# The last pair of each feed-forward's first part as seven block products

## The chip, the cores and the metric

One core of a Trainium2 chip runs the whole program. The metric is the device time of one execution in microseconds (us), as the median of several runs of the same kernel.

## What is computed

Two layers on 512 tokens of width 1024. Layer 0 has a causal convolution module, layer 1 differential attention; each is followed by a SwiGLU feed-forward network with a hidden width of 2816 and by a gated per-layer embedding. Only the two feed-forwards matter here:

```python
def swiglu(x, w_gate, w_up, w_down):
    return (jax.nn.silu(x @ w_gate) * (x @ w_up)) @ w_down

u = rms_norm(h, ffn_norm_g[i])
h = h + swiglu(u, ffn_w_gate[i], ffn_w_up[i], ffn_w_down[i])
```

All values are float32. The kernel splits every operand of a product into a rounded part (hi) and the rest (lo), and a product is three matmuls: hi by lo, lo by hi, hi by hi (`mm3`, lines 162 to 165).

## The kernel before

The activations stand with the features on the 128 partitions and the 512 tokens along the free axis, so a width of 1024 is 8 chunks of 128 x 512, and the hidden width is 22 chunks. `ffn` (it begins at line 572) takes these 22 chunks in three parts of 8, 8 and 6 (`PARTS`). A part makes its hidden chunks two at a time, a **pair**; with pairs written as (part, number) there are (0,0) to (0,3), (1,0) to (1,3) and (2,0) to (2,2), eleven in all. Then `linear` multiplies the part's chunks by the down weights and adds the result to `h` (lines 758 and 759). This second half of a part is called the down product here.

An **ordinary pair** makes, for each of its two chunks, the gate product and the up product from eight input chunks: four weights of 128 x 1024, and 4 x 8 x 3 = 96 matmuls of 512 columns. Each weight is loaded by SyncE's queue (L153), rounded on ScalarE (L156, the hi part) and its rest taken on VectorE (L158, the lo part).

A **seven-product pair** (those listed in `SEVEN`) makes the same two chunks by Strassen's scheme: input features, hidden features and tokens are each cut into two halves, and seven block products with a contraction over four chunks and 256 tokens take the place of eight. `strassen` runs once for the gate and once for the up weights, with 7 x 4 x 3 = 84 matmuls of 256 columns each, 168 for a pair. Two kinds of operands feed it:

- `comb`, sums and differences of blocks of the activations. Blocks 1, 2 and 3 are the normed activations themselves; 5, 7, 6 and 4 are made by the generator `normed` (lines 618 to 622, on VectorE and ScalarE). They are written into the tiles A, which hold the raw input `norm.u` until the last raw pair has read it.
- `operands`, sums and differences of blocks of the weights: a difference q, made by a plain load on SyncE's queue (L649) and an accumulating DMA on GpSimd's queue (L650); a raw block r (L652); a smaller block z (L654, tile `bias`); two sums s2 and s4 on VectorE (L666, L667). All of them are split by `split` (L642 on ScalarE, L643 on VectorE) into the ring of four hi and four lo tiles that the ordinary weights use as well.

The seven products run in the order 1, 5, 7, 2, 6, 4, 3; product 1 needs r, products 5 and 7 need q.

The first two ordinary pairs read `norm.u`, unnormed, and scale their results by the row factors `rb`. The later ordinary pairs read the normed tiles `un`. The generator `normed` first makes the eight normed chunks (lines 592 to 599) and then, once the raw pairs are done, the eight steps of `comb`. `feed(n)` lets it take n steps; the table `STEPS` says how many after each half of an ordinary pair, and 2 is taken where the table ends.

The order of instructions on each engine is fixed when the program is built: a scheduler places them from the order of the code and its own estimates. On the chip each engine then works through its list in order.

The sources of the normed chunks are kept in three tiles of the kinds that q uses (`qtags`: C5, C5, C4 in layer 0, C2, C3, C4 in layer 1), and in `wth`, which s2 uses. So the first q in such a tile can be loaded only when the steps of `comb` that read the old content have run.

Of the kernel before, what the change touches and what calls it, by code (L numbers as in the profile page):

```python
# [23 lines left out]
NC = D // P  # L24
# [58 lines left out]
    (("C2", "C3", "C4"), [(t,) for t in ("C0", "C0", "C1", "C1", "C5", "C5")] + [("D0", "D1"), ("D4", "D5")]),  # L83
)
RAW_PAIRS = 2
STEPS = (0, 2, 3, 3)
SEVEN = ((1,0),(1,1),(1,2),(1,3),(2,0),(2,1),(2,2))
QKV = (("q", 0, (0, 0, 0, 0)), ("v", 0, (0, 1, 1, 0)), ("q", 1, (1, 1, 2, 2)), ("q", 2, (0, 1, 2, 0)), ("v", 1, (1, 2, 2, 2)), ("q", 3, (0, 2, 0, 1)))


# [1 line left out]
def trunk(ctx, tc, xT, pT, wts, diag, dww, vec, rel, onehot, lamv, out):  # L92
# [9 lines left out]
    def sb(shape, tag, bufs, dt=F32):  # L102
        uid[0] += 1
        return pool.tile(shape, dt, tag=tag, name=f"{tag}_{uid[0]}", bufs=bufs)
# [40 lines left out]
    def weight(n=1024, pieces=1, between=(), eng=V, after=None):  # L145
        i = wnext[0]
        wnext[0] += 1
        raw = sb([P, 1024], "wraw", 2)
        hi = sb([P, 1024], "whi", 4, F32R)
        lo = sb([P, 1024], "wlo", 4, F32R)  # L150
        for k in range(pieces):
            cut = slice(k * n // pieces, (k + 1) * n // pieces)
            loaded[0] = nc.sync.dma_start(raw[:, cut], wts[i, :, cut])  # L153
            if k < len(between):
                between[k]()
            A.copy(hi[:, cut], raw[:, cut])  # L156
            with tc.issue_after(after.ins) if after else nullcontext():
                eng.tensor_tensor(lo[:, cut], raw[:, cut], f(hi[:, cut]), ALU.subtract)  # L158
        return hi, lo

    def mm3(acc, a, b, first, last):
        (ah, al), (bh, bl) = a, b
        T.matmul(acc, al, bh, start=first, stop=False)  # L163
        T.matmul(acc, ah, bl, start=False, stop=False)  # L164
        return T.matmul(acc, ah, bh, start=False, stop=last)  # L165

    def wpart(w, k):
        return tuple(t[:, k * P : (k + 1) * P] for t in w)
# [377 lines left out]
    def linear(n_in, src, consume, group0=1, before=None, after=None, first=(None,) * 3):  # L546


        m = 0
        while m < NC:  # L550
            g = group0 if m == 0 else 1
            ws = [weight(n_in * P, after=first[i] if m == 0 else None) for i in range(g)]
            accs = [mm() for _ in range(g)]
            for k in range(n_in):
                if before:
                    before(k)
                for w_, a_ in zip(ws, accs):
                    mm3(a_, wpart(w_, k), src[k], k == 0, k == n_in - 1)
                    if after:
                        after()  # L560
            for i in range(g):
                consume(m + i, accs[i])
            m += g
# [10 lines left out]
    def ffn(norm, after, space):  # L574
        qtags, utags = space
        rb = None
        un = []
        comb = {}
        uses = [None]
# [46 lines left out]
        making = [normed()]  # L626

        def feed(n=1):
            for _ in range(n):
                if making:  # L630
                    try:
                        next(making[0])
                    except StopIteration:
                        making.pop()
# [42 lines left out]
        def strassen(i):  # L677

            w = operands(i)

            def product(acc, name):
                for k in range(4):
                    mm3(acc, wpart(w[name], k), comb[name][k], k == 0, k == 3)

            one, two, three, four = sc(), mm(), mm(), tp()
            t, e, g = wk(), big(), big()
            first, second = slice(0, H2), slice(H2, S)
            product(one[:, first], 1)
            A.copy(t[:, first], one[:, first])
            A.mul(t[:, second], one[:, first], -1.0)  # L690
            product(three[:, first], 5)
            product(three[:, second], 7)
            product(two[:, first], 2)
            product(two[:, second], 6)
            V.tensor_tensor(e, two, t, ALU.add)
            V.tensor_tensor(
                g.rearrange("p (a s) -> p a s", a=2), three.rearrange("p (a s) -> p a s", a=2),
                e[:, second].unsqueeze(1).to_broadcast([P, 2, H2]), ALU.add,
            )
            V.tensor_tensor(e[:, second], three[:, second], g[:, first], ALU.add)  # L700
            product(four[:, second], 4)
            V.tensor_tensor(g[:, second], four[:, second], g[:, second], ALU.add)
            product(four[:, first], 3)
            V.tensor_tensor(g[:, first], four[:, first], g[:, first], ALU.subtract)
            return e, g

        seen = 0
        for at, (f0, n) in enumerate(PARTS):
            hid = []
            for pair in range(n // 2):  # L710
                hi, lo = (sb([P, 2, S], f"B{2 * pair + k}", 1, F32R) for k in range(2))
                for k in range(2):
                    hid.append((hi[:, k], lo[:, k]))
                if (at, pair) in SEVEN:
                    i = wnext[0]
                    wnext[0] += 4
                    gs = strassen(i)
                    for t in gs:
                        A.activation(t, t, AF.Silu)
                    us = strassen(i + 1)  # L720
                    for o, (t, g) in enumerate(zip(us, gs)):
                        V.tensor_tensor(t, t, g, ALU.mult)
                        first, step = (H2, H2) if o else (0, S + H2)
                        hs, ls = (bass.AP(x.tensor, x.offset + first, [list(x.ap[0]), [step, 2], [1, H2]]) for x in (hi, lo))
                        A.copy(hs, t.rearrange("p (a s) -> p a s", a=2))
                        V.tensor_tensor(ls, t.rearrange("p (a s) -> p a s", a=2), f(hs), ALU.subtract)
                    continue
                x = norm.u if seen < RAW_PAIRS else un
                for i in range(2):
                    wg, wu = weight(), weight()  # L730
                    pg, pu = mm(), mm()
                    for k in range(NC):
                        mm3(pg, wpart(wg, k), x[k], k == 0, k == NC - 1)
                    if rb is None:
                        norm.diagonal()
                    for k in range(NC):
                        mm3(pu, wpart(wu, k), x[k], k == 0, k == NC - 1)
                    if rb is None:
                        rb = norm.rows()
                    tg, tu = big(), big()  # L740
                    if x is un:
                        A.activation(tg, pg, AF.Silu)
                        V.tensor_tensor(tu, pu, tg, ALU.mult)
                    else:
                        V.tensor_tensor(tg, pg, rb, ALU.mult)
                        A.activation(tg, tg, AF.Silu)
                        V.tensor_tensor(tu, pu, rb, ALU.mult)
                        V.tensor_tensor(tu, tu, tg, ALU.mult)
                    A.copy(hi[:, i], tu)
                    V.tensor_tensor(lo[:, i], tu, f(hi[:, i]), ALU.subtract)  # L750
                    feed(STEPS[2 * seen + i] if 2 * seen + i < len(STEPS) else 2)
                seen += 1
                if seen == RAW_PAIRS:
                    assert len(un) == NC, len(un)
                    feed()
                    uses[0] = None

            def add(m, acc):
                V.tensor_tensor(h[m], acc, h[m], ALU.add)  # L759
                if at == len(PARTS) - 1:  # L760
                    after.chunk(m)

            linear(n, hid, add, 2)
# [28 lines left out]

    n2 = Norm("ple_g0")
    ffn(norm, n2, SPACE[0])
    norm = Norm("attn_g")
    ple(n2, pp, lambda m, cut: norm.chunk(m))
# [281 lines left out]
    linear(NC, ot, add_attn, 2, heads_until, step)  # L1078
    n2 = Norm("ple_g1")
    ffn(norm, n2, SPACE[1])  # L1080

    def store(m, cut):
# [130 lines left out]
```

## Time and profile before

| | us |
|---|---|
| median of three runs | 1290.93 |
| lowest and highest run | 1288.16, 1292.81 |
| the profiled execution | 1288.43 |
| its span, first to last instruction | 1286.3 |

The profiled execution is 2.1 us longer than its span. PE is TensorE's matmul, PEld its weight load, DVE is VectorE, ACT ScalarE, POOL GpSimd and SP SyncE, whose queue issues most DMAs. A row of the windows view gives, for one stretch of the span, its length, the busy time of each engine with the number of instructions, the granted clock of TensorE, the share of the DMA engines' time in use, and the GB/s. A row of the timeline gives the start, the time taken, the engine, the line, the operation, the tiles (out<-in) and the shapes; in brackets stands the idle time before it and what ended it. Rows of one kind that follow one another are merged into one with a count.

### The profile page before, as it was taken

The page shows a single profiled execution, that of the slowest core. Times are in us where ns is not written, and L with a number is a line of the kernel's source. Part 1 is how long each engine was busy: PE and PEld are TensorE (multiplying, and loading weights), DVE is VectorE, ACT ScalarE, POOL GpSimd, SP SyncE. Part 2 cuts the span into 40 slices and gives each one's busy share as a digit, 9 for nine tenths or more (in the row PEclk, how much of TensorE's full clock was granted, in tenths as well). Part 3 has the DMA queues.
Part 4 walks back from the last instruction along what each step waited for, and adds up shares of the span by engine and source line. Part 5 has one row for each costly group of instructions (what it writes and reads, how often), then busy time and mean ns, then how long its engine had stood idle before and what let it go on. Part 6 is the DMA issues. An engine that isn't in the chain of part 4 may idle for free. (4 is left out here: it accounts for less than half of the span.)

```text
span 1286.3 us, 18032 instructions
## 1 busy us (share of the span) xinstructions
PE 1253.5 (97%) x6912; PEld 1082.9 (84%) x6912; DVE 886.0 (69%) x1430; ACT 603.9 (47%) x999; POOL 268.4 (21%) x235
## 2 busy tenths in 40 slices
PE   8999999999999999999999997999999999999998
PEld 5888678888899989988888886778888899899887
DVE  6988647773478558766678887846953588558665
ACT  5642455442155325454566766734532255225442
POOL 4644323000000000033435534122000001000030
PEclk8999989999999999999999999999999999999999
DMA  6745314272456545243222221313463366444241
GB/s 228 226 154 167 116 49 116 81 213 82 115 155 174 148 123 134 69 127 104 80 87 92 83 64 50 98 49 116 119 175 99 105 172 175 136 113 117 81 137 66
DMA packets 58498, 154.15 MB, mean 120 GB/s; under 512 B 6275, under 2 KB 10883, under 8 KB 58412
## 3 DMA queue, kind: packets, MB, share of 16 engines
q1 hardware_dynamic: 52256, 134.89, 32.6%
q0 software_dynamic: 4032, 14.68, 6.9%
q10 hardware_dynamic: 2124, 3.43, 0.8%
q8 instruction: 54, 0.88, 0.3%
q14 instruction: 32, 0.26, 0.1%
HBM read 148.77 MB, written 4.21 MB: 119 GB/s over the span
## 5 line engine op out<-in xcount | busy, mean ns | idle before, releaser
L163 PE MATMUL mm<-A,wlo 128*128 128x512 f32 (+1 forms) x856 | 295.2, 350 | 5.6 <-ACT A L177 2.6
L164 PE MATMUL mm<-A,whi 128*128 128x512 f32 (+1 forms) x856 | 298.6, 350 | 0.3
L165 PE MATMUL mm<-A,whi 128*128 128x512 f32 (+1 forms) x856 | 296.5, 347 | 0.0
L156 ACT CAST whi<-wraw 128x1024 fp32r<-128x1024 f32 (+2 forms) x158 | 159.5, 1016 | 253.6 <-PE mm L165 120.0
L158 DVE TENSOR_TENSOR wlo<-wraw,whi 128x1024 fp32r<-128x1024 f32 (+2 forms) x154 | 196.3, 1278 | 86.3 <-ACT whi L156 86.1
L163 PEld LDWEIGHTS mm<-A,wlo 128*128 128x128 f32 x856 | 162.8, 190 | 28.5 <-DVE wlo L158 3.9
L164 PEld LDWEIGHTS mm<-A,whi 128*128 128x128 f32 x856 | 162.9, 190 | 24.2 <-DVE A L178 3.5
L165 PEld LDWEIGHTS mm<-A,whi 128*128 128x128 f32 x856 | 162.8, 190 | 20.6 <-issue 1.0
L164 PE MATMUL mm<-B,whi 128*128 128x512 f32 x352 | 137.2, 391 | 0.0
L165 PE MATMUL mm<-B,whi 128*128 128x512 f32 x352 | 137.1, 390 | 0.0
L163 PE MATMUL mm<-B,wlo 128*128 128x512 f32 x352 | 135.9, 392 | 0.0
L650 POOL DMA_DIRECT2D C<-in_wts x28 | 24.6, 878 | 520.0 <-DVE h L759 228.9
L197 POOL TENSOR_TENSOR acc<-acc,wk 128x512 f32<-128x512 f32 x42 | 66.1, 1574 | 229.2 <-ACT wk L196 121.2
L759 DVE TENSOR_TENSOR h<-mm,h 128x512 f32<-128x512 f32 x48 | 33.0, 688 | 75.2 <-PE mm L165 75.1
L165 PEld LDWEIGHTS mm<-B,whi 128*128 128x128 f32 x352 | 66.1, 188 | 14.5
L164 PEld LDWEIGHTS mm<-B,whi 128*128 128x128 f32 x352 | 66.1, 188 | 14.1
L163 PEld LDWEIGHTS mm<-B,wlo 128*128 128x128 f32 x352 | 66.1, 188 | 14.0
L165 PE MATMUL mm<-whi,A 128*128 128x512 f32 x192 | 75.7, 395 | 0.0
L164 PE MATMUL mm<-wlo,A 128*128 128x512 f32 x192 | 74.9, 395 | 0.0
L163 PE MATMUL mm<-whi,A 128*128 128x512 f32 x192 | 74.8, 396 | 0.0
L163 PE MATMUL mm<-C,wlo 128*128 128x512 f32 (+1 forms) x212 | 74.1, 350 | 0.0
L164 PE MATMUL mm<-C,whi 128*128 128x512 f32 (+1 forms) x212 | 73.8, 348 | 0.0
(269 smaller groups left out, 2593.8 us busy)
## 6 DMA issues: line engine op xcount, KB each, us to landing
wraw<-in_wts SPq DMA_DIRECT2D x166, 512.0 KB, 3.7
C<-in_wts SPq DMA_DIRECT2D x28, 512.0 KB, 4.5
C<-in_wts POOLq DMA_DIRECT2D x28, 512.0 KB, 6.0
bias<-in_wts SPq DMA_DIRECT2D x28, 256.0 KB, 3.6
wraw<-in_wts SPq DMA_DIRECT2D x16, 384.0 KB, 3.1
D<-in_diag SPq DMA_DIRECT2D x22, 256.0 KB, 4.8
C<-in_diag SPq DMA_DIRECT2D x16, 256.0 KB, 4.7
h<-in_xT SPq DMA_DIRECT2D x8, 256.0 KB, 5.8
```

What stands on the lines that cost most here:

```text
L156: A.copy(hi[:, cut], raw[:, cut])
L158: eng.tensor_tensor(lo[:, cut], raw[:, cut], f(hi[:, cut]), ALU.subtract)
L163: T.matmul(acc, al, bh, start=first, stop=False)
L164: T.matmul(acc, ah, bl, start=False, stop=False)
L165: return T.matmul(acc, ah, bh, start=False, stop=last)
L197: self.last = self.eng.tensor_tensor(self.acc, self.acc, sq, ALU.add)
L650: nc.gpsimd.dma_start(q, wts[i + 2].rearrange("p (a s) -> p a s", a=2), accum_op=ALU.add)
L759: V.tensor_tensor(h[m], acc, h[m], ALU.add)
```

## The change

The pair (0,3) of each feed-forward joins the list `SEVEN`, so that eight of eleven pairs are seven-product pairs and three are ordinary: (0,0) and (0,1) on the raw input, (0,2) on the normed one. `STEPS` now feeds the eight normed chunks during the first two pairs (2, 2, 2 and 3 steps) and the eight steps of `comb` during pair (0,2) (4 and 5 steps). Two loops take the place of a fixed assumption: what is left of `normed` is fed before the first seven-product pair, and before the raw tiles are given up.

```diff
 RAW_PAIRS = 2
-STEPS = (0, 2, 3, 3)
-SEVEN = ((1,0),(1,1),(1,2),(1,3),(2,0),(2,1),(2,2))
+STEPS = (2, 2, 2, 3, 4, 5)
+SEVEN = ((0,3),(1,0),(1,1),(1,2),(1,3),(2,0),(2,1),(2,2))
...
                 if (at, pair) in SEVEN:
+                    while making:
+                        feed()
                     i = wnext[0]
                     wnext[0] += 4
                     gs = strassen(i)
...
                 if seen == RAW_PAIRS:
-                    assert len(un) == NC, len(un)
-                    feed()
+                    while uses[0] is not un:
+                        feed()
                     uses[0] = None
```

In layer 1, VectorE's list around the end of pair (0,2) and the start of (0,3) reads before as follows (names with A are tiles of `comb`, B the hidden chunks, wlo the weights' rests; L743 multiplies a chunk's up product by its gate, L750 is the rest of a hidden chunk):

```order
L743 TENSOR_TENSOR big_8608<-mm_8558,big_8607 128x512
L158 TENSOR_TENSOR wlo_8719<-wraw_8717,whi_8718 128x1024
L622 TENSOR_TENSOR A_1721_8872<-wk_8868,A_1720_8871 128x512
L750 TENSOR_TENSOR B_1655_8544<-big_8608,B_1654_8543 128x512
L158 TENSOR_TENSOR wlo_8796<-wraw_8794,whi_8795 128x1024
L743 TENSOR_TENSOR big_8691<-mm_8641,big_8690 128x512
```

and after the change (lines from 716 on have moved down by two, so L745 and L752 are L743 and L750 of before):

```order
L745 TENSOR_TENSOR big_8734<-mm_8684,big_8733 128x512
L622 TENSOR_TENSOR A_1719_8860<-wk_8856,A_1718_8859 128x512
L752 TENSOR_TENSOR B_1675_8670<-big_8734,B_1674_8669 128x512
L666 TENSOR_TENSOR wth_8880<-C_1722_8865,wraw_8868 128x512
L666 TENSOR_TENSOR wth_9009<-C_1742_8994,wraw_8997 128x512
L667 TENSOR_TENSOR wtl_8881<-wth_8880,wraw_8868 128x512
L643 TENSOR_TENSOR wlo_8877<-C_1722_8865,whi_8876 128x1024
L667 TENSOR_TENSOR wtl_9010<-wth_9009,wraw_8997 128x512
L643 TENSOR_TENSOR wlo_8885<-wth_8880,whi_8884 128x512
L643 TENSOR_TENSOR wlo_8885<-wtl_8881,whi_8884 128x512
L745 TENSOR_TENSOR big_8830<-mm_8780,big_8829 128x512
```

The last step of `comb` (L622) keeps its place. The first sum of the new pair (L666) now stands behind it, and it reads the new pair's first q, the tile C_1722; everything below it in the list comes after that.

SyncE's list at the same place in layer 1, before (C tiles are the q blocks, L153 the ordinary weights):

```order
L649 DMA C_1798_9397<-in_wts 128x2x512
L153 DMA wraw_8634<-in_wts 128x1024
L649 DMA C_1776_9262<-in_wts 128x2x512
L153 DMA wraw_8711<-in_wts 128x1024
L153 DMA wraw_8717<-in_wts 128x1024
L649 DMA C_1756_9133<-in_wts 128x2x512
L153 DMA wraw_8794<-in_wts 128x1024
L153 DMA wraw_8800<-in_wts 128x1024
```

and after the change:

```order
L649 DMA C_1796_9385<-in_wts 128x2x512
L153 DMA wraw_8773<-in_wts 128x1024
L649 DMA C_1742_8994<-in_wts 128x2x512
L652 DMA wraw_8868<-in_wts 128x1024
L652 DMA wraw_8997<-in_wts 128x1024
L649 DMA C_1722_8865<-in_wts 128x2x512
L153 DMA wraw_9127<-in_wts 128x1024
L649 DMA C_1816_9514<-in_wts 128x2x512
```

The three q blocks are loaded at the same places as before. The two loads of raw blocks (L652) stand where two ordinary weights stood. The third q, which fed the seven-product pair after a whole down product, is now the first operand of the pair that follows at once. Outside pair (0,3) and the down product behind it, the five lists of both layers are the same as before but for a few neighbours on VectorE and ScalarE that have changed places.

## The prediction

> **What bounds the kernel now.** First the page's busy shares and its slices, to see whether one engine carries the whole span.
>
> ```profile
> PE 1253.5 (97%) x6912; PEld 1082.9 (84%) x6912; DVE 886.0 (69%) x1430; ACT 603.9 (47%) x999; POOL 268.4 (21%) x235
> PE   8999999999999999999999997999999999999998
> PEclk8999989999999999999999999999999999999999
> ```
>
> TensorE is busy for 97% of the span, and in nearly every slice for nine tenths or more, at the full granted clock but for two slices near the start. An average over stages is not yet a bound in the stage that changes, so next the windows view, cut at the borders of the pairs. I took the borders from TensorE's timeline, where the first matmul of each kind starts.
>
> ```profile
> core 0: us, PE busy (x) PEld busy (x) DVE busy (x) ACT busy (x) POOL busy (x), PEclk, DMA share, GB/s
> 264.62:286.38 21.76, 21.76 (x97) 18.02 (x96) 14.79 (x25) 8.61 (x12) 1.75 (x2) 1.00 0.86 215
> 286.38:308.14 21.76, 21.76 (x97) 18.02 (x96) 7.49 (x8) 6.22 (x8) 0.00 (x0) 1.00 0.31 98
> 308.14:352.16 44.02, 44.02 (x194) 36.05 (x192) 19.42 (x24) 8.93 (x10) 0.87 (x1) 1.00 0.33 98
> 352.16:372.31 20.15, 20.15 (x169) 20.15 (x168) 13.11 (x19) 9.98 (x16) 0.87 (x1) 1.00 0.52 129
> 352.16:432.69 80.53, 79.81 (x662) 79.35 (x660) 63.09 (x97) 42.56 (x68) 6.13 (x7) 1.00 0.63 162
> 432.69:478.18 45.49, 45.49 (x207) 37.49 (x205) 24.05 (x32) 10.60 (x12) 0.87 (x1) 1.00 0.45 130
> 478.18:537.38 59.20, 59.20 (x494) 59.08 (x493) 45.27 (x69) 30.87 (x50) 1.74 (x2) 1.00 0.37 102
> 929.96:951.72 21.76, 21.76 (x97) 18.02 (x96) 14.85 (x25) 8.62 (x12) 2.03 (x3) 1.00 0.83 214
> 951.72:973.48 21.76, 21.76 (x97) 18.02 (x96) 7.49 (x8) 6.21 (x8) 0.00 (x0) 1.00 0.30 92
> 1017.50:1037.65 20.15, 20.15 (x169) 20.15 (x168) 13.11 (x19) 9.98 (x16) 0.86 (x1) 1.00 0.49 127
> ```
>
> In order: pair (0,2) of layer 0, pair (0,3), the down product of that part, the seven-product pair (1,0), all four seven-product pairs of part 1, the down product behind them, the three pairs of part 2; then (0,2), (0,3) and (1,0) of layer 1. (A count may hold one matmul of the neighbouring window.) In every row but one TensorE is busy for the whole length, and the exception loses 0.72 of 80.53 us. So these stages are bound by TensorE, and what the change is worth is what it does to TensorE's list, as long as no operand comes late.
>
> **Pair (0,3) itself.** It takes 21.76 us in both layers: 96 matmuls at a pace of 0.227 us. A seven-product pair issues 168 matmuls of half the columns. Where operands are on time it takes 20.15 us, in both layers, a pace of 0.120 us. The change turns the first into the second once in each layer: 21.76 - 20.15 = 1.61 us, twice, **3.2 us**. Note how little is left of the 12.5% that seven for eight promises: a matmul of half the width takes 0.120 and not 0.113 us, and 168 x 0.120 stands against 96 x 0.227. PEld, the weight load, is busy for all of the 20.15 us, while it has 3.7 us to spare in the ordinary pair, so it may be what sets the pace.
>
> Seven-product pairs do not always run at that pace. Part 1 of layer 0 spends 80.53 us on 660 matmuls (0.1220), part 2 59.20 on 494 (0.1198). Over 168 matmuls these give 20.50 and 20.13, so a pair is worth between 1.26 and 1.63 us, and the two between 2.5 and 3.3. The slow bound contains one wait for a weight split:
>
> ```profile
> 413.90 0.36 PE L163 MATMUL mm<-A,wlo 128*128 128x256 f32 x1 [0.72 <-DVE wlo L643]
> ```
>
> I take 20.15, the row of the two pairs that, like (0,3), are the first of their run.
>
> **The down product behind it.** TensorE's list lets the last product of a seven-product pair (12 matmuls) run inside the following down product, among its first matmuls, as it does after part 1 now. That row, 45.49 us, less 12 x 0.12 = 1.44, leaves 44.05, against 44.02 behind an ordinary pair. I charge 0.03 per layer, **0.1 us** in all.
>
> **The steps that move.** The normed chunks and the steps of `comb` have another table, but VectorE's list keeps them at the places where they stand, so nothing is paid or won there. The matmuls of pairs (0,0) to (0,2) are the same and in the same order.
>
> **The first operands.** Before, q was loaded far ahead, and a whole down product lay between the end of `comb` and the first seven-product pair. Now pair (0,3) follows at once, and product 5, which is 12 x 0.12 = 1.44 us behind the pair's start, needs q. The chain is: the last reader of the old tile on VectorE, the plain load (SyncE), the accumulating load (GpSimd), the sums and the split on VectorE. In layer 1 it is tightest, because there the tile of the first q holds normed chunks that `comb` reads until its seventh step:
>
> ```profile
> 936.05 0.74 DVE L618 TENSOR_TENSOR wk<-C,wk 128x256 f32<-128x256 f32 x2
> 936.88 0.38 SPq L649 DMA_DIRECT2D C<-in_wts  x1
> 942.33 0.86 POOL L650 DMA_DIRECT2D C<-in_wts  x1 [9.08 <-DVE big L743]
> 943.87 0.68 DVE L750 TENSOR_TENSOR B<-big,B 128x512 fp32r<-128x512 f32 x1
> 948.11 1.22 DVE L158 TENSOR_TENSOR wlo<-wraw,whi 128x1024 fp32r<-128x1024 f32 x1 [3.55 <-ACT whi L156]
> DMA to landing us min/median/max: 5.7/5.7/5.7
> DMA to landing us min/median/max: 5.2/6.0/9.1
> DMA to landing us min/median/max: 4.8/4.8/4.8
> DMA to landing us min/median/max: 3.6/4.5/6.0
> ```
>
> The landing rows are those of this accumulating load, of all 28, of this plain load, and of all 28. The plain load starts right behind the reader, at 936.88, and takes 4.8 us. The accumulating load starts at 942.33 and lands 5.7 us later: 948.0. VectorE is idle from 944.5 to 948.1, so it reaches the first sum (L666) when q lands. Behind that stand, in its list, two more sums and then the rest of q:
>
> ```profile
> L643 DVE TENSOR_TENSOR wlo<-C,whi 128x1024 fp32r<-128x1024 f32 x7 | 8.5, 1218 | 0.4 <-ACT whi L642 0.4
> L667 DVE TENSOR_TENSOR wtl<-wth,wraw 128x512 f32<-128x512 f32 x5 | 3.4, 688 | 0.1
> L666 DVE TENSOR_TENSOR wth<-C,wraw 128x512 f32<-128x512 f32 x5 | 3.4, 685 | 3.5 <-DMA wraw<-in_wts 3.5
> ```
>
> 3 x 0.69 + 1.22 = 3.3, so q is ready at 951.3; ScalarE's rounding of q runs beside the sums. Product 5 wants it at 951.72 + 1.44 = 953.16. **1.9 us to spare.** In this time two ordinary weights that were loaded beside the accumulating load (SyncE's list has two L153 behind the q) are gone or wait for a free raw tile, so q lands earlier rather than later. The new wait stands at the head of VectorE's list. Queued behind it are the other splits of the pair; the sums are wanted by product 6, which starts 5.76 us into the pair, at 957.5, and they end at about 953.5. By the slowest landing, 9.1 us, q lands at 951.4 and is split at 954.7: 1.5 us late. Nothing earlier than in time can be won, so the bounds are 0 and 1.5 us; I take 0, by this load's own row.
>
> In layer 0 the tiles are free earlier:
>
> ```profile
> 263.43 1.05 POOL L650 DMA_DIRECT2D C<-in_wts  x1 [32.83 <-ACT A L621]
> 266.78 0.88 POOL L650 DMA_DIRECT2D C<-in_wts  x1 [2.29 <-DVE wk L618]
> ```
>
> Even at 9.1 us both first q blocks have landed by 275.9, more than ten us before pair (0,3) starts at 286.38. I charge nothing.
>
> **VectorE and the DMAs as a whole.** Pairs (0,2) and (0,3) have VectorE busy for 14.8 + 7.5 = 22.3 us of 43.5. A seven-product pair costs it 63.09 / 4 = 15.8 us in part 1, so the two would come to some 31 of 41.9. The transfers have room too: pair (0,3) uses 0.31 of the DMA engines and would go to about 0.63, the share of part 1.
>
> **The sum.** -3.2 + 0.1 = -3.1 us. Against the profiled execution that is 1288.43 - 3.1 = 1285.3, of which the span is 1283.2 and 2.1 lie around it. The median of the runs shown stands 2.5 us above the profiled execution; from it, 1290.93 - 3.1 = **1287.8 us**, 0.24% less. A measurement of this kernel tells about 0.3% (3.9 us) from no change, since its runs spread over 4.65 us, so a real gain of this size is likelier to be called the same than faster.
>
> **The rivals.** (1) *The first q is late.* TensorE then waits at product 5 of layer 1: 1.5 us with the slowest accumulating load, and 1.2 more if the plain load before it takes 6.0 instead of 4.8 us. The time is then 1289.3 to 1290.5. For it speaks that accumulating loads took up to 9.1 us where three of them crowded (263 us); against it that this one has already been seen at 5.7 us among two weight loads. [...]
>
> (2) *Slower than before.* The same place, but a landing so late that it eats the whole gain. VectorE stands still at the first sum and the whole pair waits with it, one us for each us. q must land by 953.16 - 3.3 = 949.9; the gain of 3.1 us is gone when it lands at 953.0, 10.7 us after its issue. At twice the median, 12 us, it lands at 954.3: 4.4 us late, 1290.93 - 3.1 + 4.4 = 1292.2. The slowest of 28 is 9.1, so this has little chance.
>
> (3) *Half the columns take half the time.* Were the pace of the new blocks 0.227 / 2 = 0.1133 us, the pair would take 19.04, the gain would be 2 x 2.72 = 5.4 us, and the time 1285.5. Every seven-product row speaks against it. [...]
>
> (4) *The change does not take place*, or the scheduler gives the pair back elsewhere: 1290.9. The built lists exclude the first: TensorE has 144 matmuls more, 72 per layer, and (0,3) stands there as 256-column blocks.
>
> **How the numbers follow.** My forecast has 0.80, the late q 0.12, slower 0.04, half time 0.02, no gain 0.02. The range takes in the pair's worth at 0.1220 us (2.5 instead of 3.2) and the late q above, and on both sides the spread of the runs themselves: 1288.16 - 3.1 = 1285.1 and 1292.81 - 2.5 = 1290.3. I go a little beyond, to 1284.5 and 1291.3. Faster by over 0.3% needs 1287.06 or less, 0.7 us under my forecast: a third of the forecast's chance, and the half-time case, 0.31. Slower by over 0.3%, above 1294.8, takes a wait of 7 us, the far end of rival 2, or half of it and an unlucky median: 0.02. The rest, 0.67, lies within.
>
> **What would show it.** Right: in the profile after, 21.76 us becomes about 20.15 between the last matmul of pair (0,2) and the first of the down product, with 12 matmuls of the last product among the down product's first; no wait on TensorE at the first product with tile A in layer 1 (about 953 us); the later stages shifted as a block, by 1.6 us after layer 0's pair and by 3.1 after layer 1's. Wrong: a wait there that ends on L643; a wait for a weight split in the down product behind (0,3), whose raw tiles now come free only as the pair's sums are done; or other idle gaps in parts 1 and 2, whose loads shift against each other.

## The result and the profile after

| | before | after |
|---|---|---|
| median, us (6 runs each, taken side by side) | 1292.51 | 1284.82 |
| lowest and highest run | 1288.16, 1293.21 | 1281.57, 1287.34 |
| the profiled execution | 1288.43 | 1285.64 |
| its span | 1286.3 | 1283.8 |

The ratio is 0.9944, with a 95% interval from 0.9923 to 0.9964: 7.2 us less, between 4.7 and 10.0. Predicted were 3.1 less and a time of 1287.8, in a range from 1284.5 to 1291.3. The two profiled executions differ by only 2.8 us. So there are two questions: whether the pair does what was said, and why the medians differ by more.

The page of the kernel after, busy shares and slices:

```profile
PE 1253.2 (98%) x7056; PEld 1089.0 (85%) x7056; DVE 910.9 (71%) x1470; ACT 614.0 (48%) x1019; POOL 273.5 (21%) x239
PE   8999899999999999999999998999999999999998
PEclk8999989999999999999999999999999999999999
```

TensorE has 144 matmuls more, and its busy time is the same within 0.3 us. The totals hide the gain: up to pair (0,2) of layer 0 TensorE is busy for 251.86 us in the kernel before and for 254.45 in the kernel after, in the same 1198 matmuls, and behind it for 2.9 us less. What the windows view of the kernel after says of the places that the prediction spoke of (columns as before: length, busy time of PE, PEld, DVE, ACT and POOL with counts, granted clock, DMA share, GB/s):

```profile
267.41:289.17 21.76, 21.76 (x98) 18.02 (x96) 17.18 (x30) 8.81 (x13) 2.46 (x3) 1.00 0.78 202
289.17:307.88 18.71, 18.71 (x158) 18.71 (x156) 11.10 (x16) 9.46 (x15) 1.04 (x2) 1.00 0.61 131
307.88:353.37 45.49, 45.49 (x207) 37.49 (x205) 24.17 (x32) 10.60 (x12) 0.88 (x1) 1.00 0.45 130
353.37:432.74 79.37, 79.37 (x662) 79.25 (x660) 63.39 (x97) 42.69 (x68) 6.15 (x7) 1.00 0.65 163
929.18:950.94 21.76, 21.76 (x98) 18.02 (x96) 14.98 (x27) 8.71 (x13) 1.73 (x2) 1.00 0.65 155
950.94:969.65 18.71, 18.71 (x157) 18.71 (x156) 13.23 (x20) 9.44 (x16) 1.72 (x2) 1.00 0.65 178
969.65:1015.14 45.49, 45.49 (x206) 37.50 (x205) 24.11 (x32) 10.59 (x12) 0.86 (x1) 1.00 0.46 131
```

In order: pair (0,2), pair (0,3), the down product and the pairs of part 1 in layer 0, then the first three of these in layer 1. Pair (0,2) is unchanged. Pair (0,3) takes 18.71 us up to the first matmul of the down product, with 156 of its 168 matmuls. The other twelve stand inside the down product, as TensorE's timeline of the kernel after shows:

```profile
314.48 0.39 PE L165 MATMUL mm<-B,whi 128*128 128x512 f32 x1
314.71 0.28 PE L163 MATMUL tp<-C,wlo 128*128 128x256 f32 x1
```

At 12 x 0.12 = 1.44 us they make the pair 20.15 us, the predicted number, in both layers. The down product is 45.49 us with them and 44.05 without, as predicted too. Taken together, pair and down product go from 65.78 us (21.76 + 44.02) to 64.20 (18.71 + 45.49). No row loses a tenth of a microsecond on TensorE.

The first q of layer 1, in the timeline of the kernel after (the landing rows are those of the plain load and of the accumulating one):

```profile
936.11 0.38 SPq L649 DMA_DIRECT2D C<-in_wts  x1
942.81 0.86 POOL L650 DMA_DIRECT2D C<-in_wts  x1 [10.64 <-DVE A L622]
DMA to landing us min/median/max: 6.1/6.1/6.1
DMA to landing us min/median/max: 5.6/5.6/5.6
948.40 1.29 DVE L666 TENSOR_TENSOR wth<-C,wraw 128x512 f32<-128x512 f32 x2 [4.87 <-DMA C<-in_wts]
949.61 0.69 DVE L667 TENSOR_TENSOR wtl<-wth,wraw 128x512 f32<-128x512 f32 x1
950.22 1.22 DVE L643 TENSOR_TENSOR wlo<-C,whi 128x1024 fp32r<-128x1024 f32 x1
952.37 0.28 PE L163 MATMUL mm<-A,wlo 128*128 128x256 f32 x1
```

VectorE stands idle for 4.87 us, in the place foreseen, and q is split at 951.44. TensorE comes for it at 952.37 and does not wait. But only 0.93 us were to spare, not 1.9: the plain load took 6.1 us where the same load took 4.8 before, and so the accumulating one started later. (The row names L622 as what it waited for; but in the kernels before and after and in two of the experiments it starts 0.6 us behind the landing of the plain load, whatever the row names.)

Where the two spans differ (2.5 us) shows when the same matmul is looked up in both traces. Up to pair (0,2) of layer 0 the kernel after is 2.8 us late; pair (0,3) brings 1.6; part 1 takes 79.37 us instead of 80.53, 1.1 to 1.2 less, since the wait that the prediction quoted (413.90) is not there; between the two feed-forwards another 0.9 has gone, in the attention; the second pair (0,3) brings 1.6. 2.8 - 1.6 - 1.1 - 0.9 - 1.6 = -2.4; the last 0.1 lies behind the feed-forward of layer 1 (+0.1 up to the last matmul, -0.2 from there to the end). The first and the fourth lie in stages whose lists are the same in both kernels but for a few neighbours. The first goes with the granted clock, 150 to 170 us, of the kernel before and of the kernel after; the second row is in each the first matmul behind a wait of TensorE in this stretch:

```profile
150.00:170.00 20.00, 16.85 (x71) 12.62 (x70) 10.86 (x19) 6.47 (x13) 6.87 (x7) 0.83 0.17 49
156.78 0.50 PE L163 MATMUL mm<-wth,wlo 128*128 128x512 f32 x1 [2.25 <-ACT D L275]
```

```profile
150.00:170.00 20.00, 16.74 (x58) 12.90 (x57) 8.37 (x15) 4.89 (x10) 4.47 (x4) 0.63 0.14 39
156.01 0.79 PE L163 MATMUL mm<-wth,wlo 128*128 128x512 f32 x1 [3.26 <-ACT D L275]
```

In the same 20 us TensorE is granted 0.83 of its clock in the one and 0.63 in the other, and gets through 71 and 58 matmuls. Behind the wait of 2.25 us matmuls of 512 columns follow one another at 0.23 to 0.24 us, behind that of 3.26 at 0.43. In the thirteen profiles of this document, the stretch of 100 matmuls around it takes 31.9 to 35.0 us where this wait is 3.0 us or longer (five profiles), and 27.5 to 31.1 where it is shorter (eight). Such waits come and go from execution to execution, so one pair of profiles can't carry the medians' 7 us.

### The profile page after: what moved, and what is told of

The parts are those of the page before. It is cut to its first block, busy times and chain, and to the rows that moved or that the text cites. A ratio compares the mean times of both kernels' runs of the same rounds, so it can differ in the third digit from the quotient of the medians.

```text
span 1283.8 us, 18407 instructions
## 1 busy us (share of the span) xinstructions
PE 1253.2 (98%) x7056; PEld 1089.0 (85%) x7056; DVE 910.9 (71%) x1470; ACT 614.0 (48%) x1019; POOL 273.5 (21%) x239
## 5 line engine op out<-in xcount | busy, mean ns | idle before, releaser
L164 PE MATMUL mm<-A,whi 128*128 128x512 f32 (+1 forms) x904 | 312.7, 347 | 0.6 <-DVE A L178 0.3
L163 PE MATMUL mm<-A,wlo 128*128 128x512 f32 (+1 forms) x904 | 308.3, 346 | 4.5 <-DVE wlo L158 2.5
L165 PE MATMUL mm<-A,whi 128*128 128x512 f32 (+1 forms) x904 | 310.0, 344 | 0.0
L156 ACT CAST whi<-wraw 128x1024 fp32r<-128x1024 f32 (+2 forms) x150 | 151.2, 1014 | 233.0 <-PE mm L165 93.4
L158 DVE TENSOR_TENSOR wlo<-wraw,whi 128x1024 fp32r<-128x1024 f32 (+2 forms) x146 | 186.6, 1280 | 65.8 <-ACT whi L156 65.0
L163 PEld LDWEIGHTS mm<-A,wlo 128*128 128x128 f32 x904 | 171.8, 190 | 27.5 <-DVE wlo L158 4.2
L164 PEld LDWEIGHTS mm<-A,whi 128*128 128x128 f32 x904 | 172.1, 190 | 24.5 <-DVE A L178 3.8
L165 PEld LDWEIGHTS mm<-A,whi 128*128 128x128 f32 x904 | 172.1, 190 | 20.4 <-issue 1.0
L650 POOL DMA_DIRECT2D C<-in_wts x32 | 28.1, 880 | 511.4 <-DVE h L761 179.4
L164 PEld LDWEIGHTS mm<-B,whi 128*128 128x128 f32 x352 | 66.1, 188 | 13.9
L222 POOL TENSOR_TENSOR r<-v,mhalf 128x8 f32<-128x8 f32 (+1 forms) x31 | 46.2, 1490 | 117.1 <-DVE v L220 94.6
L643 DVE TENSOR_TENSOR wlo<-wraw,whi 128x1024 fp32r<-128x1024 f32 x32 | 39.2, 1225 | 32.8 <-ACT whi L642 32.8
```

The costliest lines, as they stand in the source:

```text
L222: last_pow[0] = G.tensor_tensor(r[:, :n], v[:, :n], mhalf[:, :n], ALU.pow)
L643: V.tensor_tensor(lo, raw, f(hi), ALU.subtract)
L650: nc.gpsimd.dma_start(q, wts[i + 2].rearrange("p (a s) -> p a s", a=2), accum_op=ALU.add)
```

## The experiments

Theory A: TensorE's list is shorter by 1.6 us per layer, and the rest of the 7 us is the spread of other stages. Theory B: the change is worth some 2 us more, steadily, in a place that the prediction left out. The measurements, each against the kernel before on the same chip:

| kernel | median | before beside it | ratio, 95% interval |
|---|---|---|---|
| after, first measurement | 1284.82 | 1292.51 | 0.9944 (0.9923 to 0.9964) |
| after, second | 1287.22 | 1291.53 | 0.9955 (0.9938 to 0.9971) |
| after, third | 1284.95 | 1289.65 | 0.9965 (0.9948 to 0.9982) |
| after, with the old table of steps | 1286.53 | 1290.70 | 0.9969 (0.9957 to 0.9981) |
| layer 1 alone | 1288.55 | 1291.53 | 0.9970 (0.9953 to 0.9988) |
| layer 0 alone | 1287.66 | 1289.65 | 0.9984 (0.9972 to 0.9996) |
| (0,3) in, (2,2) out | 1287.93 | 1291.53 | 0.9978 (0.9962 to 0.9993) |
| the new table alone | 1291.40 | 1290.70 | 1.0010 (0.9998 to 1.0021) |
| before, against itself | 1290.20 | 1291.53 | 0.9995 (0.9979 to 1.0011) |
| (0,3) and part 2, none of part 1 | 1300.13 | 1290.70 | 1.0086 (1.0068 to 1.0103) |
| nine pairs | 1313.57 | 1290.91 | 1.0174 (1.0150 to 1.0198) |

**The changed kernel again**, unaltered.

> The changed kernel once more. Theory A (the change takes 1.6 us out of TensorE's list in each layer, and the rest of the first measurement's 7 us is the spread of stages that the change does not touch): 3 to 4 us faster than before, ratio 0.9970, and in the profile 20.15 us for each pair (0,3), with the time to the start of pair (0,2) of layer 0 anywhere between 264 and 268 us. Theory B (the change also shortens a stage outside pair (0,3)): 7 us faster again, ratio 0.9944, with a stage that is shorter by the same amount in every profile of the changed kernel.

0.9955, 5.8 us less; the interval holds both theories. Both pairs (0,3) take 18.71 us again up to the down product. And a third time, later:

> The changed kernel once more, unaltered, beside the other half of the layer test. Theory A (TensorE's list is shorter by 1.6 us per layer and nothing else): a ratio of 0.9976, 3.1 us less. Theory B (the eighth pair also spares some further 2 us, somewhere outside the pair): about 0.9960, 5.1 us less, as the mean of the three measurements so far has it (0.9944, 0.9955 and, with the old table, 0.9969).

0.9965, 4.5 us less, between the two theories, and again the interval holds both. The kernel before, against itself, shows how far such a ratio strays when nothing is changed:

> The kernel before, unchanged, measured against itself. Both theories: ratio 1.000. Theory A: its profile differs from the first one of before by up to 4 us in the convolution stage (to the start of pair (0,2) of layer 0 at 264.62 us), with the same instruction lists, and not in the feed-forwards. Theory B: the convolution stage repeats within 1 us.

0.9995. Its profile decides nothing between the theories: the start of pair (0,2) came at 265.56 us, 0.9 from the first profile's, which is within what either said. The feed-forward of layer 0, which theory A let stand, was 1.1 us shorter, without the wait at 413.90, and the attention 1.6 longer. The medians of the kernel before in the five measurements run from 1289.65 to 1292.51; the first had the highest, which is part of its 7 us.

**One layer at a time.** In layer 1 alone, and then, with `SPACE[0]` in the same line, in layer 0 alone:

```diff
-                if (at, pair) in SEVEN:
+                if (at, pair) in SEVEN and ((at, pair) != (0, 3) or space is SPACE[1]):
```

> Pair (0,3) as seven products in layer 1 alone, ordinary in layer 0. Theory A: half of the gain, 1.6 us, ratio 0.9988; in the profile 21.76 us for (0,3) of layer 0 and 20.15 for that of layer 1. Theory B: between 3 and 4 us if the further effect goes with each pair, or all of it if it sits in one layer.

> Pair (0,3) by seven products in layer 0 alone, ordinary in layer 1. Theory A: half the gain, 1.6 us, a ratio of 0.9988, with 40.5 us from pair (0,2) to the down product in layer 0 and 43.5 in layer 1. Theory B: half of its 5 us, 0.9980; with layer 1 alone 0.9970 was measured, so that the two halves should give the whole of the unaltered kernel measured beside them.

The windows of pair (0,3) in layer 0 and in layer 1, first with layer 1 alone, then with layer 0 alone:

```profile
288.93:310.69 21.76, 21.76 (x98) 18.02 (x96) 7.49 (x8) 6.22 (x8) 0.00 (x0) 1.00 0.30 99
953.59:972.30 18.71, 18.71 (x157) 18.71 (x156) 12.46 (x19) 9.36 (x15) 1.72 (x2) 1.00 0.71 190
```

```profile
285.86:304.57 18.71, 18.71 (x158) 18.71 (x156) 11.09 (x16) 9.46 (x15) 1.09 (x2) 1.00 0.58 135
947.51:969.27 21.76, 21.76 (x98) 18.02 (x96) 7.49 (x8) 6.22 (x8) 0.00 (x0) 1.00 0.34 98
```

The pair is 21.76 or 18.71 us, wherever it stands, and the feed-forward around it does not answer: from the first matmul of (0,2) to the first one behind the last down product, the layer with the pair takes 304.16 and 304.15 us and the layer without it 305.73 and 305.72, 1.57 apart. The ratios give 3.9 and 2.1 us; both intervals hold theory A's 1.6, the first only just, and both hold what theory B expected.

**The same number of pairs, elsewhere.** (0,3) joins and (2,2) leaves, so TensorE has as many matmuls of each kind as before.

```diff
-SEVEN = ((0,3),(1,0),(1,1),(1,2),(1,3),(2,0),(2,1),(2,2))
+SEVEN = ((0,3),(1,0),(1,1),(1,2),(1,3),(2,0),(2,1))
```

> Pair (0,3) as seven products and the last pair of part 2, (2,2), ordinary again: seven of eleven pairs, as before, at another place. Theory A: no difference from before, ratio 1.000, within 1 us in the touched stages. Theory B, if the further effect comes with (0,3): 3 to 5 us faster.

In its trace (2,2) takes 21.8 us again, so what one pair gains the other loses; each feed-forward takes 305.6 us where the kernel before, without its wait, has 305.7. The time should have been the same and is 2.8 us less, between 0.9 and 4.9. This speaks against theory A alone. But it is no clean test: in this kernel the lists of TensorE, VectorE and ScalarE in the attention (812 to 835 us in the kernel before) are in another order too.

**The table of steps.** The new table with the old list, and the old table with the new list:

```diff
-STEPS = (0, 2, 3, 3)
+STEPS = (2, 2, 2, 3, 4, 5)
```

> The new table of feeds with the old list of seven-product pairs, (0,3) ordinary. The lists of the engines are nearly those of before. Theory A (1.6 us for each pair that becomes seven products, in TensorE's list, and nothing else): ratio 1.000; in the profile 21.76 us for both pairs (0,3). Theory B (some 1.5 to 2 us come on top with the new build, whatever the number of pairs): 1.5 to 2 us faster than before, ratio 0.9987.

```diff
-STEPS = (2, 2, 2, 3, 4, 5)
+STEPS = (0, 2, 3, 3)
```

> The changed list of pairs with the old table of feeds (the loop before the first seven-product pair feeds what is left). Theory A: as the change, 3.2 us faster than before, ratio 0.9975, with 20.15 us for both pairs (0,3); the table itself is worth nothing. Theory B: 5 us faster, ratio 0.9961. Rival to both: without the new table comb comes later, and TensorE waits at product 5 of (0,3) for several us.

The table alone is worth nothing (1.0010, and theory B's 0.9987 lies outside the interval), and without it the list keeps its gain (4.0 us, with both theories inside the interval). In its profile both pairs (0,3) take 18.71 us up to the down product, without a wait, so its rival is out: but for single neighbours the scheduler puts the steps in the same places either way, as the prediction had it. The loops that feed what is left make the table unnecessary.

**Fewer pairs.** (0,3) and part 2 stay, the four of part 1 become ordinary: three fewer per layer than before.

```diff
-SEVEN = ((0,3),(1,0),(1,1),(1,2),(1,3),(2,0),(2,1),(2,2))
+SEVEN = ((0,3),(2,0),(2,1),(2,2))
```

> The four pairs of part 1 ordinary again, (0,3) and part 2 as seven products: four pairs of eleven, against seven before and eight after the change. Theory A: three pairs less than before in each layer, 6 x 1.6 = 9.7 us slower than before, ratio 1.0075. Theory B with a larger worth per pair (2.5 us): 15 us slower, ratio 1.0116; with a fixed gain of the build: 8 us slower, ratio 1.006.

Measured 1.0086, 11.1 us slower, between 8.8 and 13.3. The interval holds the count's 9.7 and leaves out both of theory B's numbers, but it rests on four runs, 1294.36, 1298.66, 1301.60 and 1301.94 us, whose mean is only 8.7 above that of the kernel before. So it does not decide about a fixed bonus (1.006). About a larger worth of every pair (1.0116) the trace does: the feed-forwards take 310.37 and 310.38 us instead of 305.73, 9.3 more in all and 1.55 for each pair. Here too the lists in the attention are in another order.

**How near the first q is to being late.** Its plain load is issued a second time behind the first, so that the accumulating load waits for both. The operands keep their values.

```diff
+            if turn[0] == 1:
+                nc.sync.dma_start(q, bass.AP(wts.tensor, wts.offset + i * P * 1024, [[1024, P], [2 * P * 1024, 2], [1, S]]))
```

> The changed kernel with the plain load of the first q in each layer issued twice, the second waiting for the first. That puts about 5 us into the chain that ends with q. In the profile after, q's split in layer 1 ends at 951.44 us and product 5 starts at 952.37, so 0.9 us are spare; in layer 0 it ends at 282.2 and product 5 starts at 290.6, 8.4 us spare. If that chain is what would bind: TensorE waits about 4 us at the first matmul with tile A of pair (0,3) in layer 1, not at all in layer 0, and the kernel is 4 us slower than after. Rival (q is not on the way of product 5, or has far more to spare): no wait in either layer.

SyncE's, GpSimd's, VectorE's and TensorE's rows of this kernel in layer 1, and the window behind the wait:

```profile
932.80 0.38 SPq L649 DMA_DIRECT2D C<-in_wts  x1
938.86 0.38 SPq L651 DMA_DIRECT2D C<-in_wts  x1
943.27 0.86 POOL L652 DMA_DIRECT2D C<-in_wts  x1 [14.60 <-DMA C<-in_wts]
948.75 1.29 DVE L668 TENSOR_TENSOR wth<-C,wraw 128x512 f32<-128x512 f32 x2 [9.32 <-DMA C<-in_wts]
950.56 1.22 DVE L643 TENSOR_TENSOR wlo<-C,whi 128x1024 fp32r<-128x1024 f32 x1
951.83 0.39 PE L163 MATMUL mm<-A,wlo 128*128 128x256 f32 x1 [2.61 <-DVE wlo L643]
951.83:956.00 4.17, 4.17 (x34) 4.17 (x35) 3.65 (x6) 2.04 (x4) 0.00 (x0) 1.00 0.72 255
```

Counted from the start of pair (0,2) (925.87 us here, 929.18 after), q is split at 951.78 - 925.87 = 25.91 where it was 951.44 - 929.18 = 22.26: 3.65 later. Less the 0.93 to spare, 2.7 us of waiting are due, and TensorE loses 2.77 between its pace and the first product with A. Layer 0 has no wait. So the chain is the one named, and beyond its spare time its delay came through whole. The wait is shorter than the 4 us expected because the second load landed in 3.8 us and not in 5. In the single run the time was 1285.39, although 4 us more than after were expected: pair (0,2) of layer 0 began at 263.77 us here and at 267.41 after, so another stage hid the loss, and one run says nothing of it.

**Nine pairs.** Pair (0,2), under which the sums and the first q are made, becomes a seven-product pair too.

```diff
-SEVEN = ((0,3),(1,0),(1,1),(1,2),(1,3),(2,0),(2,1),(2,2))
+SEVEN = ((0,2),(0,3),(1,0),(1,1),(1,2),(1,3),(2,0),(2,1),(2,2))
```

> Pair (0,2), the only pair on normed operands that is still ordinary, becomes a seven-product pair as well: nine of eleven. This takes away the cover under which the eight steps of the activation sums and the first q stand ready: they now have to be made between the end of the raw pairs and the first product that needs them. Theory A says that a pair is worth 1.61 us per layer only where its operands are on time, so the two further pairs would bring 3.2 us and the missing cover costs more: waits on TensorE at the first products of (0,2), ending on the sums of activations or on the weight split behind them, of about 8 to 14 us in layer 0 and 15 to 20 in layer 1 (there the q chain of the profile after, 15.5 us from the plain load to the end of the split, starts only when the sums have been read). Together some 20 us over the changed kernel, a ratio to before of 1.013 to 1.020. Theory B, that the list of TensorE alone decides and operands come early enough anyway, says 3.2 us less than the changed kernel: a ratio of about 0.993 to 0.995, and no wait at the first products.

1.0174, 22.5 us slower. The windows of (0,2) and (0,3) together in each layer, then TensorE at product 5 of (0,2) in both layers and the loads of layer 1's first q:

```profile
269.07:317.39 48.32, 41.09 (x326) 40.48 (x325) 38.95 (x63) 24.65 (x40) 5.25 (x6) 0.96 0.75 188
939.46:996.10 56.64, 41.23 (x326) 41.03 (x324) 39.36 (x63) 24.67 (x40) 5.20 (x6) 0.85 0.66 161
275.31 0.58 PE L163 MATMUL mm<-A,wlo 128*128 128x256 f32 x1 [4.65 <-DVE wlo L643]
956.46 0.58 PE L163 MATMUL mm<-A,wlo 128*128 128x256 f32 x1 [15.41 <-DVE wlo L643]
941.71 0.75 DVE L618 TENSOR_TENSOR wk<-C,wk 128x256 f32<-128x256 f32 x2
942.55 0.37 SPq L649 DMA_DIRECT2D C<-in_wts  x1
947.89 0.86 POOL L650 DMA_DIRECT2D C<-in_wts  x1 [7.29 <-DMA C<-in_wts]
953.38 1.29 DVE L666 TENSOR_TENSOR wth<-C,wraw 128x512 f32<-128x512 f32 x2 [7.23 <-DMA C<-in_wts]
```

The plain load can start only behind the last step of `comb` that reads its tile, at 942.5, when TensorE has been waiting for a microsecond and a half. From there the chain runs through, load, accumulating load, sums and split: 13.9 us to product 5. The two pairs take 48.32 and 56.64 us where the kernel after takes 40.47 (21.76 + 18.71): 7.9 and 16.2 more, although their list is 1.6 shorter: 9.5 and 17.8 us are lost, as theory A had it.

## Why the prediction was right, and where it was small

**The pair.** Right to the hundredth: 21.76 became 20.15 us, in both layers, in the two single-layer kernels, and where four pairs were taken out. The pace of a 256-column matmul is 0.120 us, and the rival of half the time has no row behind it. Two slips did not touch the forecast. Part 2 holds 492 matmuls and not 494 (two of the count belong to the neighbouring windows), so its pace is 0.1203 us and a pair's worth between 1.26 and 1.55 us. And a 9 in the slices of the clock says 90% or more; that the clock was full in the feed-forwards is read from the windows' 1.00. The weight load is busy for all of the 18.71 us as well; whether it sets the pace, as the prediction thought possible, was not tried.

**The down product and the moved steps.** Right: 44.05 us, and a table that moves nothing but single neighbours.

**VectorE and the DMAs.** Room enough, as said: the DMA share in pair (0,3) is 0.61 and 0.65 (0.63 was estimated). VectorE is busy for 28.2 of the 40.47 us in layer 1 (14.98 + 13.23) and 28.3 in layer 0 (17.18 + 11.10); the estimate of 31 in 41.9 also holds what now falls into the down product.

**The first operands.** Right in outcome and chain, too large in its margin. "1.9 us to spare" took the plain load at the 4.8 us of its own row; it took 6.1, a little over the slowest of 28 before, and that put off the accumulating load's start by 1.3. Of the two things that the rival of the late q reckoned with, the smaller one did happen, a plain load of 6.0 us; the larger, an accumulating load of 9.1 us, did not. (Of the three loads that "crowded" before, only two overlapped, those issued at 263.43 and 266.78 us, with 9.1 and 8.8 us to landing; the third, at 278.08, was issued when both had landed and took 7.2. What makes such a load take 5.2 or 9.1 us no run shows.) "q lands earlier rather than later" holds for the accumulating load alone (5.6 us instead of 5.7); against the pair's start q landed 1.2 us later. The new neighbours in SyncE's list are not what lengthened the plain load: in the kernel with the pair in layer 0 alone, where SyncE's list in layer 1 is that of before, it took 6.4 us, and in the kernel with (2,2) out, which has the new neighbours, 5.3. In the six profiles in which layer 0 has one seven-product pair more than before it took 5.8 to 6.4 us, in five of the other six with this load in the same place 4.6 to 5.3 and in one, with layer 1 alone, 5.7. Why is open. That no wait came is in part luck: 0.9 to 1.6 us were to spare in the three profiles of the changed kernel, and with the two loads as they landed with the pair in layer 0 alone (6.4 and 7.4 us) product 5 of layer 1 would have waited for about 1.2. This is an estimate: from the start of (0,2), the accumulating load at 13.93, 7.4 to its landing and 3.0 to the end of the split make 24.4, and product 5 is due at 23.2.

**The sum.** The trace bears out -3.1 us, and the measured change is larger. Weighted by their intervals, the three measurements and the one with the old table give a ratio of 0.9961, from 0.9954 to 0.9969: 5.0 us, between 4 and 6. The mis-sized term is the one that the sum doesn't have: it let all other stages stand.

A small part is located. The time around the span is 2.14 to 2.15 us, as a mean over the runs, in the kernel before and with the table alone, and 1.77 to 1.82 in every kernel with the new pair that keeps (2,2), 0.3 to 0.4 less; and from the last matmul to the last instruction it is 4.73 us in three profiles without the new pair (before, twice, and the table alone) and 4.49 or 4.50 in four with it (after, three times, and the old table). The cause of neither was looked for. Of the rest, 0.3 to 2.3 us, two things can be said.

It isn't in the feed-forwards. From (0,2) to the end of the last down product a layer without the pair takes 305.72 to 305.97 us in every profile that has neither wait nor another list there, and a layer with it 304.15 or 304.16. What comes on top are waits: 1.1 us at 413.9 in the kernel before, absent when that same kernel was profiled again; 0.5 in layer 0 and 2.6 in layer 1 in the changed kernel with the old table. And there is one place outside in which the profiles part with the change. It is a stretch of 100 matmuls in the attention, with the same lists in all the kernels named here:

```profile
795.78:823.07 27.29, 19.77 (x101) 16.45 (x101) 25.03 (x68) 21.05 (x48) 7.55 (x7) 0.81 0.47 135
DMA to landing us min/median/max: 5.2/5.2/5.2
```

```profile
795.99:822.22 26.23, 20.12 (x101) 16.47 (x101) 25.25 (x68) 20.92 (x48) 7.57 (x7) 0.80 0.46 141
DMA to landing us min/median/max: 4.6/4.6/4.6
```

First the kernel before, then the kernel after; the second row is the landing of the second weight load in the stretch. With the pair ordinary in layer 0 (before, twice, the table alone, layer 1 alone) the stretch takes 27.3 to 29.4 us and that load 5.2 to 5.5. With it as a seven-product pair (after, three times, the old table, layer 0 alone, q loaded twice) it takes 26.1 to 28.3 us, 1.6 less as a mean, and the load 4.4 to 4.9. Around it, from one feed-forward to the other, all stretches agree within 0.2 us. This is of the size that is missing, but it is one execution of each kernel, found after the fact, and why that load lands sooner was not tried: the rest stays **open**.

A bonus of the loops and the table alone is out, by the kernel that has them without the pair (1.0010), and so is a larger worth of the pairs themselves, by the feed-forwards. In the convolution the profiles are spread from 263.8 to 269.1 us at pair (0,2) and do not part with the change, which is too much scatter to show a mean of 1 or 2.

**The median.** So 1287.8 stood 0.6 to 3.0 us above the three medians. The first of them lies in the given range by 0.3 us, which is partly luck: the base that the forecast was taken from, 1290.93, was 1292.51 in the side-by-side runs, and the measured change was more than twice the forecast one. The kernel is faster by more than the 0.3% that a measurement can tell, where "within 0.3%" had twice the chance.

## What to carry to other kernels

Where one engine is busy to the last tenth in a stage, a change to its list is priced by the pace of rows already in the trace, to the hundredth, and not by the ratio of the arithmetic: seven for eight brought 7.4% of the pair and not 12.5. What decides how far such a change can go is the stage that covers the making of its operands: with one ordinary pair as cover 0.9 to 1.6 us were left, and without it the pairs (0,2) and (0,3) of both layers lost 24 us against this kernel. A gain of 3 us in 1290 is smaller than what untouched stages do from run to run (pair (0,2) of layer 0 began between 263.8 and 269.1 us), so it is shown by the trace and by edits of one layer, and the first median alone would have taken it for more than twice as much.

## What the runs showed of the hardware

TensorE's granted clock was about half behind some waits and full behind others. After 2.61 us without work (the kernel with the doubled load) the clock stayed at 1.00 and the next matmuls kept their pace of 0.12 us. After 4.65 us (nine pairs, layer 0) the next 13 started 0.21 us apart instead of 0.12, and the clock was 0.83 over the 9.50 us from there. After 15.41 us (nine pairs, layer 1) the next 24 ran at a clock of 0.53:

```profile
956.46:961.55 5.09, 5.09 (x24) 5.09 (x25) 3.74 (x6) 0.00 (x0) 0.00 (x0) 0.53 0.73 251
961.55:996.10 34.55, 34.55 (x291) 34.55 (x289) 25.85 (x39) 18.58 (x29) 3.47 (x4) 1.00 0.68 166
```

24 matmuls took 5.09 us, 2.2 more than at 0.120 each, so this wait cost more than its length. The full pace was back 3.35 us behind the wait of 4.65 and 4.85 us behind that of 15.41. The wait behind which the pace halves is not one sharp length here: in the convolution, 512-column matmuls ran at 0.43 us behind waits of 2.68 (the doubled load) and of 3.24 to 3.30 us (three profiles), and at 0.23 behind one of 2.74 (the table alone).

The same load of 512 KB, at the same place in the program, took 4.8 us before, while the DMA engines moved 340 GB/s, and 6.1 after, while they moved 240: less traffic did not make it faster, and a chain of two loads that is planned with less than 2 us to spare (1.9 planned, 0.93 left) is not safe by one row of a trace.
